# Spread's evacuation order, the first transfers and the last block's halves in a two-block transformer kernel

## The chip, the cores and the metric

The kernel runs on one core of one Trainium2 chip. The metric is the device time of one execution in microseconds (us). Five engines work side by side, each through its own queue in order: TensorE (PE) multiplies into PSUM, VectorE (DVE) and ScalarE (ACT) compute on SBUF and PSUM, GpSimd (POOL) and SyncE (SP) issue transfers here. SyncE and ScalarE both issue transfers between HBM and SBUF. [...]

## The reference, cut to what matters

The program computes two transformer blocks over 512 tokens of width 1024 in fp32. The first is norm, projections, chunked attention and a gated convolution, an output projection and a feed-forward part. The second is a modulated mixer and PEER, a layer of 16384 experts of which each token picks 128. The parts that the change touches are the very first projection and PEER:

```python
def rms_norm(x, g):
    y = xf * lax.rsqrt(jnp.mean(xf * xf, axis=-1, keepdims=True) + EPS)
    return (y * g.astype(jnp.float32)).astype(x.dtype)
...
h = rms_norm(x, norm1_g)
proj = jnp.einsum('bsd,de->bse', h, w_in)
...
# peer: 8 heads pick 16 of 128 keys twice, then 16 of the 256 pairs
idx = best_i.reshape(nb, PEER_TOKEN_BLOCK, n_sel)      # expert = i * 128 + j
gs = gate.reshape(nb, PEER_TOKEN_BLOCK, n_sel)
u = jnp.take(expert_u, ib, axis=0)
act = jax.nn.gelu(jnp.einsum('td,tkd->tk', xb, u).astype(jnp.float32), approximate=False)
vv = jnp.take(expert_v, ib, axis=0)
return jnp.einsum('tk,tkd->td', (gb * act).astype(h.dtype), vv)
```

## The kernel before

Every fp32 product of a weight and an activation is made of three matmuls: both factors are split into a high part (fp32r) and a low part, and `mm3` (lines 154 to 156) multiplies high by high, low by high and high by low. A weight tile of 1 MB comes in by one transfer on SyncE (`weights`, line 140), ScalarE makes the high part (line 143, one copy of 128x2048), VectorE the low part (line 145). The tile framework orders the instructions of each engine by its own schedule; what the change moves is told below. Each transfer takes one of eight semaphores in turn, and the one that takes a semaphore again waits for the transfer that had it, so that no more than eight of SyncE's and ScalarE's transfers are under way.

**Start.** `setup` loads two constants (`cst`, an identity and a block of ones, line 89; `vec`, all gains and biases, line 91) on SyncE. `block1` then takes the eight tiles of x (transposed, 128x512, line 285) on SyncE and the first weight in eight pieces of 128x256 on ScalarE (line 286), a piece and a tile at a time. For each, ScalarE multiplies x with its gain out of `vec` (line 229, the high part `hh`), VectorE makes the low part `lh` (line 230), ScalarE casts the weight's piece (line 289), VectorE makes its low part (line 290). The first 48 matmuls (`linear2`, both 128-column halves of a piece, piece by piece) need both; the next 48 use the weight `w_in[20]`, which comes in one transfer. Then come the column sums of x squared (lines 220 and 221).

**Spread.** For 384 of the 512 tokens every expert is computed densely, and the gates are laid out as a matrix of experts by tokens. `spread` makes that matrix: for 16 tokens at a time VectorE builds one-hot rows of the two keys (`oi` for i, `oj` for j, lines 1328 and 1330) and of j times the gate's high and low half (`oh`, `ol`, lines 1332 and 1334), each with two buffers. Per token PE multiplies `oh` by `oi` and adds `ol` by `oi` (lines 1340 and 1341), 128x128 each, four tokens in a bank; the banks are taken in turn from three tags (`c` and `d` with one bank, `b` with two, which also takes the transposes at the head of each block of 128 tokens). ScalarE copies a bank into `stage` (line 1343), a tile of 128 keys j by 128 keys i by 32 tokens, and after 32 tokens `stage` goes to HBM (line 1349, 2 MB). 96 copies are made. Between them, `ahead` computes the first 48 expert chunks' activations: 80 steps of six matmuls here, with their weights' casts (lines 143 and 145) and a gelu per chunk on ScalarE. After spread come the remaining steps of `ahead`, then the token rows (line 1101) and the first loads of gates (line 1396) and activations (line 1387) for `experts`.

**End.** `experts` walks 128 chunks. `products` (lines 1435, 1436 and 1439) adds six matmuls per chunk and block of 128 tokens, three for each half of the 1024 output columns. The last four chunks are taken block by block for the three blocks; behind each block, `tail` multiplies each half's sum with the second gate (line 1423), adds x (line 1424) and stores it (line 1425).

Of the kernel before, what the change touches and what calls it, by code (L numbers as in the profile page):

```python
# [8 lines left out]
F32 = mybir.dt.float32  # L9
# [12 lines left out]
P = 128  # L22
# [47 lines left out]
class Ker:  # L70
# [12 lines left out]
    def setup(self, es):  # L83
        nc, I = self.nc, self.I
        self.cp = es.enter_context(self.pool("cp"))
        self.raws = None
        self.table, self.table_load, self.table_users = None, None, []
        cst = self.cp.tile([P, 2 * P], F32, name="cst")
        nc.sync.dma_start(cst, I["consts"][:, 0:2 * P])
        vec = self.cp.tile([P, V_W], F32, name="vec")  # L90
        nc.sync.dma_start(vec, I["vecs"])
        self.vec = vec
        self.ident, self.bone = cst[:, 0:P], cst[:, P:2 * P]
        self.ones = self.cp.tile([P, P], F32, name="ones")
        nc.vector.memset(self.ones, 1.0)
        self.mod = self.cp.tile([P, 48], F32, name="mod")

    def act(self, out, x, func, **kw):
# [165 lines left out]
    def block1(self, es_x):  # L264
# [5 lines left out]
        with ExitStack() as es:  # L270
# [9 lines left out]
            with self.pool("n1") as tp:  # L280
                x0, hs = [], []
                raw, hi, lo = self.weight_tiles()
                for k in range(KO):
                    xt = tp.tile([P, T], F32, name=f"x0_{k}")
                    nc.sync.dma_start(xt, I["x"][k])
                    nc.scalar.dma_start(raw[:, k, :], I["w_in"][16][:, k, :])
                    x0.append(xt)
                    hs.append(self.gain_tile(hp, xt, self.v(V_N1 + k), "h1", KO))
                    nc.scalar.copy(hi[:, k, :], raw[:, k, :])
                    nc.vector.tensor_sub(lo[:, k, :], raw[:, k, :], hi[:, k, :].bitcast(F32))  # L290
                nc.vector.tensor_scalar_mul(bgh, self.v(V_BG, 16), 0.5)
                pcs = self.linear2((hi, lo), hs)
                pxs = self.linear2(self.weights(I["w_in"][20]), hs)
                acc = None
                for k in range(KO):
                    acc = self.sum_sq(tp, acc, x0[k])
                self.rsqrt(tp, self.col_sums(acc), 1.0 / D, out=rstd)
                nc.vector.tensor_mul(rstd2, rstd, rstd)
                pt = self.psum("c", 1)
                for i in range(4):  # L300
                    nc.tensor.transpose(pt[:, i * P:(i + 1) * P], rstd[:, i * P:(i + 1) * P], self.ident)
                nc.vector.tensor_copy(rtok, pt.rearrange("p (a b) -> p a b", b=P)[:, :, 0])
# [992 lines left out]
    def spread(self, kp, Ix, Jx, gate, g_dram, ahead, fetch):  # L1295
# [5 lines left out]
        with self.pool("oh", bufs=2) as tp:  # L1301
# [5 lines left out]
            for tb in range((TD + P - 1) // P):  # L1307
                if tb == 1:
                    next(fetch)
                pt = self.psum("b", 2)  # L1310
                for i, src in enumerate((Ix, Jx, gate)):
                    t = nc.tensor.transpose(pt[:, i * P:(i + 1) * P], src[:, tb, :], self.ident)
                    if tb == 0:
                        self.behind(t, after)
                ij = tp.tile([P, 2, P, 2], F16, name="oh_t")
                nc.scalar.copy(ij.rearrange("p a b c -> p (a b) c"), pt[:, :2 * P].unsqueeze(2).to_broadcast([P, 2 * P, 2]))
                gs = tp.tile([P, P], F32, name="oh_g", bufs=1)
                nc.scalar.activation(gs, pt[:, 2 * P:3 * P], AF.Copy, scale=2.0 ** 14)
                gh = tp.tile([P, 2, P, 2], F16, name="oh_w", bufs=1)
                gs = gs.unsqueeze(2).to_broadcast([P, P, 2])  # L1320
                nc.vector.tensor_copy(gh[:, 0], gs)
                nc.vector.tensor_sub(gh[:, 1], gs, gh[:, 0])
                for t0 in range(0, min(P, TD - tb * P), G):
                    if t0 % TB == 0:
                        stage = tp.tile([P, P, TB], F32, name="oh_s")
                    bc = lambda t: t[:, t0:t0 + G].unsqueeze(2).to_broadcast([P, G, P // 2, 2])
                    oi = tp.tile([P, G, P], F16, name="oh_i", bufs=2)
                    nc.vector.tensor_tensor(rows(oi), iota, bc(ij[:, 0]), op=ALU.is_equal)
                    oj = tp.tile([P, G, P], F16, name="oh_j", bufs=2)
                    nc.vector.tensor_tensor(rows(oj), iota, bc(ij[:, 1]), op=ALU.is_equal)  # L1330
                    oh = tp.tile([P, G, P], F16, name="oh_h", bufs=2)
                    nc.vector.tensor_mul(rows(oh), rows(oj), bc(gh[:, 0]))
                    ol = tp.tile([P, G, P], F16, name="oh_l", bufs=2)
                    nc.vector.tensor_mul(rows(ol), rows(oj), bc(gh[:, 1]))
                    for f in range(G // 4):
                        pg = self.psum("cdb"[nb % 3])
                        nb += 1
                        for i in range(4 * f, 4 * f + 4):
                            o = pg[:, (i % 4) * P:(i % 4 + 1) * P]
                            nc.tensor.matmul(o, oh[:, i, :], oi[:, i, :], start=True, stop=False)  # L1340
                            nc.tensor.matmul(o, ol[:, i, :], oi[:, i, :], start=False, stop=True)
                        o = t0 % TB + 4 * f
                        nc.scalar.activation(stage[:, :, o:o + 4].rearrange("p i t -> p t i"),  # L1343
                                             pg.rearrange("p (t i) -> p t i", t=4), AF.Copy, scale=2.0 ** -14)
                        n = (tb * P + t0) // 4 + f
                        for _ in range((n + 1) * left // (TD // 4) - n * left // (TD // 4)):
                            next(ahead, None)
                    if (t0 + G) % TB == 0:
                        nc.sync.dma_start(g_dram[(tb * P + t0) // TB], stage)
# [6 lines left out]
    def experts(self, es, hs, x_dram, g_dram, a_dram, rows):  # L1356
# [67 lines left out]
                nc.vector.tensor_add(o, t, o)  # L1424
                nc.sync.dma_start(self.y[b][:, half * T:(half + 1) * T], o)

        def products(b, n, v):

            mm = nc.tensor.matmul
            bc = slice(b * P, (b + 1) * P)  # L1430
            hi, lo = (t[:, bc] for t in ws[n])
            c = n % 2
            for half in range(2):
                hc = slice(half * T, (half + 1) * T)
                mm(sums[b][half], hi, v[0][:, c, hc], start=n == 0, stop=False)  # L1435
                mm(sums[b][half], hi, v[1][:, c, hc], start=False, stop=False)  # L1436
            for half in range(2):
                hc = slice(half * T, (half + 1) * T)
                mm(sums[b][half], lo, v[0][:, c, hc], start=False, stop=n == P - 1)  # L1439

# [19 lines left out]
            down_weights(p)  # L1460
        for _ in rows:
            pass
        for b in range(nb):
            for n in range(last, P):
                products(b, n, down[n // 2])
            tail(b)


def _tiled(w, ko=KO):
# [77 lines left out]
```

## Time and profile before

| what | value |
|---|---|
| median of 3 runs | 2550.01 us (2549.26 to 2550.56) |
| the profiled execution | 2545.76 us, its span 2544.0 us |
| PE busy | 2478.2 us, 97% of the span |
| DVE busy | 1868.4 us, 73% |
| ACT busy | 1098.0 us, 43% |
| PE's first matmul | 7.59 us |
| the 96 copies of spread | 1502.59 to about 1647 us |
| PE's last matmul ends | about 2538.3 us |

The page gives busy time by engine, the span in 40 slices, the chain of work that ended last, and the costliest groups of instructions; a group's line number is that of the source. The trace can be asked for the instructions of any stretch in order, for waits (who waited for whom, in total, how often, and the longest), and for each engine's busy time in a stretch. All times in it are from the profiled execution. Engines are idle in front of an instruction until what it waits for is there; the releaser stands behind an arrow.

### The profile page before, as it was taken

The numbers are of one execution on the slowest core, as the hardware profiler recorded it, in microseconds if no ns is written. First come the engines' busy times: TensorE is split into PE (matmuls) and PEld (weight loads), VectorE is DVE, ScalarE is ACT, GpSimd is POOL, SyncE is SP. The second block draws the span as 40 slices with busy tenths as digits, with TensorE's granted clock in tenths as the row PEclk, the third lists the DMA queues.
The fourth block names the chain that finished last, engine by engine and source line by source line (L and its number), as shares of the span: only waits on it lengthen the run. The fifth ranks groups of instructions, "written<-read, shape, count | busy, mean of one in ns | idle before, by whom it ended". The sixth has DMA issues, their size and how long they took to land. (4 is left out here: it accounts for less than half of the span.)

```text
span 2544.0 us, 33077 instructions
## 1 busy us (share of the span) xinstructions
PE 2478.2 (97%) x12637; PEld 2114.3 (83%) x12637; DVE 1868.4 (73%) x3094; ACT 1098.0 (43%) x1479; POOL 627.2 (25%) x506
## 2 busy tenths in 40 slices
PE   8999999999999999999999998999999999999999
PEld 6887887877888878777788987878889999999998
DVE  5558777755555557896779998767767877888887
ACT  5226555643222136666643357743333333333332
POOL 0001100111001001101045630011145555555552
PEclk9999999999999999999999999999999999999999
DMA  5353222443443441114343456799879999999995
GB/s 196 131 197 101 100 92 100 152 167 145 157 151 138 149 137 68 55 54 159 111 155 116 127 221 250 279 332 335 300 261 331 329 330 328 332 327 333 331 334 188
DMA packets 172312, 515.03 MB, mean 202 GB/s; under 512 B 13396, under 2 KB 78308, under 8 KB 146296
## 3 DMA queue, kind: packets, MB, share of 16 engines
q1 hardware_dynamic: 133960, 376.52, 41.9%
q0 software_dynamic: 37040, 135.35, 14.8%
q8 instruction: 99, 1.62, 0.2%
q10 hardware_dynamic: 1152, 1.05, 0.1%
q14 instruction: 61, 0.50, 0.1%
HBM read 461.47 MB, written 51.38 MB: 202 GB/s over the span
## 5 line engine op out<-in xcount | busy, mean ns | idle before, releaser
L143 ACT CAST whi<-wraw 128x2048 fp32r<-128x2048 f32 x229 | 437.7, 1911 | 545.2 <-PE pa L155 315.8
L145 DVE TENSOR_TENSOR wlo<-wraw,whi 128x2048 fp32r<-128x2048 f32 x210 | 489.0, 2329 | 131.4 <-ACT whi L143 126.5
L154 PE MATMUL pa<-hh,whi 128*128 128x512 f32 (+1 forms) x1360 | 522.6, 384 | 12.4 <-ACT hh L229 10.5
L155 PE MATMUL pa<-lh,whi 128*128 128x512 f32 (+1 forms) x1360 | 520.5, 383 | 0.0
L156 PE MATMUL pa<-hh,wlo 128*128 128x512 f32 (+1 forms) x1360 | 517.7, 382 | 1.2 <-DVE wlo L290 1.2
L1145 POOL DMA_INDIRECT r_row<-in_u_rows,r_at x128 | 190.2, 1486 | 467.2 <-DVE r_w L1166 430.6
L154 PEld LDWEIGHTS pa<-hh,whi 128*128 128x128 f32 x1360 | 256.3, 189 | 57.3 <-ACT hh L229 10.9
L1435 PE MATMUL pp<-whi,hew 128*128 128x512 f32 x768 | 299.2, 391 | 3.0 <-ACT whi L143 1.6
L1436 PE MATMUL pp<-wlo,hew 128*128 128x512 f32 x768 | 299.7, 391 | 1.4 <-DVE wlo L145 1.4
L155 PEld LDWEIGHTS pa<-lh,whi 128*128 128x128 f32 x1360 | 256.3, 188 | 44.0 <-issue 6.1
L156 PEld LDWEIGHTS pa<-hh,wlo 128*128 128x128 f32 x1360 | 255.9, 188 | 43.6 <-issue 3.6
L1145 POOL DMA_INDIRECT r_row<-in_expert_v,r_at x128 | 195.1, 1524 | 175.8 <-DVE r_big L1174 139.4
L1439 PE MATMUL pp<-whi,lew 128*128 128x512 f32 x768 | 237.2, 390 | 0.0
L154 PE MATMUL pu<-hh,whi 128*128 128x384 f32 x640 | 217.0, 339 | 0.0
L156 PE MATMUL pu<-hh,wlo 128*128 128x384 f32 x640 | 216.7, 339 | 0.0
L155 PE MATMUL pu<-lh,whi 128*128 128x384 f32 x640 | 216.4, 338 | 0.0
L1435 PEld LDWEIGHTS pp<-whi,hew 128*128 128x128 f32 x768 | 144.1, 188 | 32.2 <-ACT whi L143 2.1
L1439 PEld LDWEIGHTS pp<-whi,lew 128*128 128x128 f32 x768 | 144.1, 188 | 30.3 <-DVE lew L1403 0.2
L1436 PEld LDWEIGHTS pp<-wlo,hew 128*128 128x128 f32 x768 | 144.0, 188 | 29.8 <-DVE wlo L145 1.8
L1174 DVE SCALAR_TENSOR_TENSOR r_big<-r_row,r_w,r_big 128x1024 f32<-128x1024 f32 x127 | 162.9, 1283 | 3.0
L1402 ACT CAST hew<-ex_w 128x384 fp32r<-128x384 f32 x128 | 65.5, 513 | 228.7 <-DVE ex_w L1398 144.6
L1166 DVE CUSTOM_DVE_ANT_0 r_row<-r_row,r_big 128x1024 f32<-128x1024 f32 x128 | 151.3, 1220 | 0.0
(437 smaller groups left out, 4515.4 us busy)
## 6 DMA issues: line engine op xcount, KB each, us to landing
wraw<-in_expert_u SPq DMA_DIRECT2D x64, 1024.0 KB, 7.3
wraw<-in_expert_v SPq DMA_DIRECT2D x64, 1024.0 KB, 7.6
wraw<-in_w_in SPq DMA_DIRECT2D x37, 1024.0 KB, 4.8
ada_w<-in_w_ada SPq DMA_DIRECT2D x24, 1024.0 KB, 4.8
gate_dram<-oh_s SPq DMA_DIRECT2D x12, 2048.0 KB, 7.2
ex_g<-gate_dram SPq DMA_DIRECT2D x31, 768.0 KB, 11.3
wraw<-in_w_up SPq DMA_DIRECT2D x16, 1024.0 KB, 6.0
wraw<-in_w_down SPq DMA_DIRECT2D x16, 1024.0 KB, 4.7
```

What stands on the lines that cost most here:

```text
L143: nc.scalar.copy(hi, raw)
L145: nc.vector.tensor_sub(lo, raw, hi.bitcast(F32))
L154: mm(out, wh, xh, start=start, stop=False)
L155: mm(out, wh, xl, start=False, stop=False)
L156: return mm(out, wl, xh, start=False, stop=stop)
L1145: self.nc.gpsimd.indirect_dma_start(t, None, src, at)
L1166: later(nc.vector.tensor_tensor_reduce(row, row, h, 1.0, 0.0, op0=ALU.mult, op1=ALU.add, accum_out=w[:, k:k + 1]))
L1174: later(nc.vector.scalar_tensor_tensor(acc, row, w[:, k:k + 1], acc, op0=ALU.mult, op1=ALU.add))
L1402: nc.scalar.copy(hi, w)
L1435: mm(sums[b][half], hi, v[0][:, c, hc], start=n == 0, stop=False)
L1436: mm(sums[b][half], hi, v[1][:, c, hc], start=False, stop=False)
L1439: mm(sums[b][half], lo, v[0][:, c, hc], start=False, stop=n == P - 1)
```

## The change

Four things are changed.

1. **Evacuation in spread.** The copy from a PSUM bank to `stage` is the same 512 values, walked in another order: before, token by token with the 128 keys innermost (PSUM read in order, one value written every 128 bytes); after, key by key with the four tokens innermost (PSUM read with 512 bytes from value to value, four neighbouring values written, then a jump of 128 bytes to the next four).
2. **First transfers.** SyncE takes x's first tile, then `vec`, then the other seven tiles, then `cst`. The gains and casts stand in a loop of their own behind all transfers. A copy of one column of ones is put on ScalarE at the head.
3. **Products of ones at first.** Nine fp32 matmuls of the 128x128 tile of ones by itself go into a PSUM bank before the first real matmul; nothing reads them.
4. **Last block's halves in turn.** For the third block of tokens the last four chunks are taken for the first 512 columns, then for the other 512.

```diff
-        nc.sync.dma_start(cst, I["consts"][:, 0:2 * P])
         vec = self.cp.tile([P, V_W], F32, name="vec")
-        nc.sync.dma_start(vec, I["vecs"])
+        self.fixed = ((vec, I["vecs"]), (cst, I["consts"][:, 0:2 * P]))
...
         nc.vector.memset(self.ones, 1.0)
+        nc.scalar.copy(self.cp.tile([P, 1], F32, name="first"), self.ones[:, 0:1])
...
                 raw, hi, lo = self.weight_tiles()
+                pt = self.psum("c", 1)
+                for _ in range(9):
+                    nc.tensor.matmul(pt[:, :P], self.ones, self.ones, start=True, stop=True)
                 for k in range(KO):
                     xt = tp.tile([P, T], F32, name=f"x0_{k}")
                     nc.sync.dma_start(xt, I["x"][k])
                     nc.scalar.dma_start(raw[:, k, :], I["w_in"][16][:, k, :])
                     x0.append(xt)
+                    if k == 0:
+                        nc.sync.dma_start(*self.fixed[0])
+                nc.sync.dma_start(*self.fixed[1])
+                for k, xt in enumerate(x0):
                     hs.append(self.gain_tile(hp, xt, self.v(V_N1 + k), "h1", KO))
...
-                        nc.scalar.activation(stage[:, :, o:o + 4].rearrange("p i t -> p t i"),
-                                             pg.rearrange("p (t i) -> p t i", t=4), AF.Copy, scale=2.0 ** -14)
+                        nc.scalar.activation(stage[:, :, o:o + 4], pg.rearrange("p (t i) -> p i t", t=4), AF.Copy,
+                                             scale=2.0 ** -14)
...
-        def products(b, n, v):
+        def products(b, n, v, halves=(0, 1)):
...
-            for half in range(2):
+            for half in halves:
...
-        for b in range(nb):
+        for b in range(nb - 1):
             for n in range(last, P):
                 products(b, n, down[n // 2])
             tail(b)
+        for half in range(2):
+            for n in range(last, P):
+                products(nb - 1, n, down[n // 2], (half,))
+        tail(nb - 1)
```

On ScalarE at the start, the order with the semaphores that a row waits for (`DMAHW` and a number is one of the eight of the transfers, `wraw` a piece of the first weight, `hh` a gain). Before:

```order
L286 DMA wraw<-in_w_in 128x256 x4
L286 DMA wraw<-in_w_in 128x256 [waits DMAHW0_49]
L289 ACT_TABLE_LOAD
L289 CAST whi<-wraw 128x256
L229 ACTIVATE hh_97<-x_0_94,vec 128x512 [waits DMAHW5_49,DMAHW3_49]
L229 ACTIVATE hh_106<-x_1_103,vec 128x512 [waits DMAHW7_49]
L289 CAST whi<-wraw 128x256 [waits DMAHW2_49]
```

The same place after. The semaphores 0, 1, 3, 5 and 6 are there those of x's first tile, the first piece, x's second tile, x's third tile and the third piece; 2 is that of `vec`.

```order
L289 DMA wraw<-in_w_in 128x256
L95 ACT_TABLE_LOAD
L95 COPY first<-ones 128x1 [waits DVE_49]
L289 DMA wraw<-in_w_in 128x256 x2
L289 DMA wraw<-in_w_in 128x256 [waits DMAHW0_49]
L289 DMA wraw<-in_w_in 128x256 [waits DMAHW1_49]
L289 DMA wraw<-in_w_in 128x256 [waits DMAHW3_49]
L289 DMA wraw<-in_w_in 128x256 [waits DMAHW5_49]
L289 DMA wraw<-in_w_in 128x256 [waits DMAHW6_49]
L229 ACTIVATE hh_130<-x_0_104,vec 128x512 [waits DMAHW2_49]
L296 CAST whi<-wraw 128x256
```

All eight pieces' transfers stand ahead of the first gain now, and five of them wait for an earlier transfer; before, five stood there, one of them with a wait, and three came among the gains.

On VectorE at the end of the program, the last block's rows (`ex_t` is the sum times the gate, `y2` the block's rows of x). Before:

```order
L1423 TENSOR_TENSOR ex_t_21829<-pp_15073,y4_14943 128x512
L1423 TENSOR_TENSOR ex_t_21833<-pp_15074,y4_14943 128x512
L1424 TENSOR_TENSOR y2_14941<-ex_t_21829,y2_14941 128x512
L1424 TENSOR_TENSOR y2_14941<-ex_t_21833,y2_14941 128x512
L1543 UNCONDITIONAL_BRANCH
```

After, with `pp_15085` the first half's sum and `pp_15086` the second's:

```order
L1430 TENSOR_TENSOR ex_t_21841<-pp_15085,y4_14955 128x512
L1431 TENSOR_TENSOR y2_14953<-ex_t_21841,y2_14953 128x512
L1430 TENSOR_TENSOR ex_t_21845<-pp_15086,y4_14955 128x512
L1431 TENSOR_TENSOR y2_14953<-ex_t_21845,y2_14953 128x512
L1554 UNCONDITIONAL_BRANCH
```

The first half's two rows stand together now, ahead of the second half's. PE's last 24 matmuls are the same, the 12 of the first half ahead of the 12 of the second. In spread no row changes its place on any engine; only the shape of ScalarE's 96 copies does, from 128x4x128 to 128x128x4.

## Rows read from the trace of the kernel before

**Rows 1.** The page's first part: busy time of the engines, share, instructions.

```profile
PE 2478.2 (97%) x12637; PEld 2114.3 (83%) x12637; DVE 1868.4 (73%) x3094; ACT 1098.0 (43%) x1479; POOL 627.2 (25%) x506
```

**Rows 2.** Stretches: length, busy us of each engine (instructions), granted clock, DMA, GB/s.

```profile
0.00:12.00 12.00, 4.41 (x10) 3.19 (x11) 4.99 (x11) 6.64 (x12) 0.55 (x6) 1.00 0.79 264
12.00:34.00 22.00, 20.78 (x89) 16.12 (x88) 12.42 (x16) 12.38 (x18) 0.20 (x2) 1.00 0.47 170
34.00:100.00 66.00, 66.00 (x290) 53.76 (x289) 40.18 (x46) 22.14 (x21) 8.24 (x9) 1.00 0.44 162
1495.00:1647.00 152.00, 134.68 (x1242) 122.44 (x1241) 132.32 (x113) 117.80 (x131) 5.54 (x4) 1.00 0.68 268
1690.00:2544.00 854.00, 848.47 (x4153) 757.96 (x4151) 665.14 (x734) 288.83 (x302) 371.82 (x247) 1.00 0.89 314
```

**Rows 3.** Groups on ACT by shape: count, busy us, mean ns, idle before.

```profile
L1343 ACT ACTIVATE oh_s<-pc 128x512 f32<-128x512 f32 x32 | 36.7, 1146 | 9.9 <-PE pc L1341 4.6 <-issue 3.5 <-ACT ex_a L110 1.0
...
L1343 ACT ACTIVATE oh_s<-pd 128x512 f32<-128x512 f32 x32 | 35.8, 1120 | 8.6 <-PE pd L1341 8.6
...
L1101 ACT COPY y<-pu 128x512 f32<-128x512 f32 x10 | 5.6, 587 | 1.9 <-PE pu L1100 1.9
```

**Rows 4.** PE's waits from 1495 to 1662 us: total, times, longest.

```profile
PE pd L1340 <- ACT oh_s L1343: 8.9, 15, 1.3
PE pc L1340 <- ACT oh_s L1343: 6.1, 14, 0.7
```

**Rows 5.** DVE's waits from 1495 to 1647 us.

```profile
DVE oh_i L1328 <- PE pc L1341: 6.8, 4, 3.7
DVE oh_i L1328 <- PE pd L1341: 3.6, 2, 3.3
DVE oh_w L1321 <- ACT oh_g L1318: 2.6, 1, 2.6
```

**Rows 6.** In order of time, PE in spread: start, us, what, idle before it.

```profile
1503.71 0.22 PE L1340 MATMUL pc<-oh_i,oh_h 128*128 128x128 f16 x1 [0.38 <-ACT oh_s L1343]
```

**Rows 7.** Groups on DVE by shape: sums over runs of 8 and 4 fp16.

```profile
L1223 DVE TENSOR_TENSOR tk_e<-tk_e 128x2048 f16<-128x2048 f16 x4 | 7.8, 1948 | 0.1
...
L1223 DVE TENSOR_TENSOR tk_e<-tk_e 128x1024 f16<-128x1024 f16 x4 | 5.9, 1480 | 0.1
```

**Rows 8.** In order of time, the first 35 us, of several engines.

```profile
0.84 0.17 DVE L95 MEMSET ones<- 128x128 f32 x1 [0.84 <-PEq L1539]
...
1.67 6.60 SPq L285 DMA_DIRECT2D x<-in_x  x8
...
6.82 0.72 ACT L229 ACTIVATE hh<-x,vec 128x512 fp32r<-128x512 f32 x1 [1.04 <-DMA x<-in_x]
...
7.59 0.80 PE L154 MATMUL pa<-hh,whi 128*128 128x512 f32 x1 [7.59 <-ACT hh L229]
7.77 0.72 ACT L229 ACTIVATE hh<-x,vec 128x512 fp32r<-128x512 f32 x1 [0.23 <-DMA x<-in_x]
...
10.13 0.33 ACTq L286 DMA_DIRECT2D wraw<-in_w_in  x1
...
12.18 0.40 PE L155 MATMUL pa<-lh,whi 128*128 128x512 f32 x1
...
16.39 0.41 ACT L289 CAST whi<-wraw 128x256 fp32r<-128x256 f32 x1 [3.60 <-DMA wraw<-in_w_in]
...
33.78 1.02 PE L220 MATMUL pa<-cs_a,ones 128*128 128x512 f32 x2
```

**Rows 9.** PE behind an idle stretch in the second block, and its granted clock.

```profile
1046.39 0.80 PE L543 MATMUL pd<-sb_wh,vv 128*128 128x512 f32 x1 [3.36 <-DVE sb_wh L864]
...
1047.00:1048.00 1.00, 1.00 (x3) 0.50 0.00 0
```

**Rows 10.** In order of time, DVE behind PE's last matmul.

```profile
2538.28 1.29 DVE L1423 TENSOR_TENSOR ex_t<-pp,y 128x512 f32<-128x512 f32 x2 [2.95 <-PE pp L1439]
2539.49 1.28 DVE L1424 TENSOR_TENSOR y<-ex_t,y 128x512 f32<-128x512 f32 x2
```

More of the change, by code (lines that the diff above doesn't have):

```diff
@@ L1436, in products @@
                 mm(sums[b][half], hi, v[1][:, c, hc], start=False, stop=False)
-            for half in range(2):
+            for half in halves:
                 hc = slice(half * T, (half + 1) * T)
```

## The prediction

> **What bounds the kernel now.** I read the page's busy shares first, then a table of stretches, then the waits and the order of time in the three places that the diff touches. TensorE (PE) is busy 97% of the span [rows 1], and the stretches tell where it is not: from 34 to 100 us it never stops, from 1690 to the end it works 848.5 of 854 us, but it has 7.6 us without work before its first matmul, loses more until 34 us, and works only 134.7 of the 152 us in which spread runs [rows 2]. So the time is PE's, and a change is worth what it takes out of PE's gaps, at the start, in spread, and behind the last matmul. The weights stream at 314 GB/s in the last stretch without holding PE up [rows 2].
>
> **Spread's evacuation.** 96 times ScalarE (ACT) copies a PSUM bank of 512 values into the stage. Now it reads in order and writes each value 128 bytes from the last one: 1146 and 1120 ns a copy; a copy of the same size that writes in order takes 587 ns [rows 3]. The changed form writes runs of four values (16 bytes) and reads PSUM with 512 bytes from value to value. Same values, same count, same place in every queue.
> The write side: no ACT row writes such runs. The nearest are VectorE (DVE) sums over every second run: 2048 values in runs of 16 bytes take 1948 ns, 1024 values in runs of 8 bytes still 1480 [rows 7]; halving the run saves a quarter, so it is runs that cost there, and runs of 16 bytes stay under a nanosecond per value. I take the write as cured.
> The read side is the open price: no row reads many values across PSUM. Its lower end is 587 ns; as upper end I take what the write costs now, about 1130 ns, since one value per step across SBUF is the nearest thing the rows show. I take 590 to 650. Nothing in the rows shows PSUM slower than SBUF to an engine that takes one value at a time, and TensorE fills those banks with 512 values every 0.23 us (66.00 us for 290 matmuls [rows 2]), more than twice ACT's pace. That reason is thin, so the upper end stays in the range.
> [...]
> What it is worth: the copies release PE's banks. PE waits 8.9 + 6.1 = 15.0 us for them, in 29 waits of 0.52 us on average [rows 4]. A copy that is 0.5 us shorter closes such a wait: at 1503.71 it is one of 0.38 us behind a single copy [rows 6]. Where three copies stand in a row it takes off more. But then DVE is late, not PE: DVE needs 132.3 us of the same 152 [rows 2] against PE's 134.7, and has waited 6.8 + 3.6 us for PE to free its one-hot buffers and 2.6 us for a small ACT copy that stood behind four evacuations [rows 5], 13.0 in all. That bounds the gain from above: 13 us by DVE, 15 by PE. Weight casts stay in ACT's queue between the copies, so not every wait goes; I take three quarters of 13, **10 us**, bounds 0 and 14. The cover of DVE's passes is gone then: a pass that is late costs its full delay.
> The gain is not given back behind spread: the loads of gates and activations for the first expert chunks are queued behind the end of the same PE work and move with it, and afterwards PE is full.
>
> **The start.** Before: x's first tile is third in SyncE's queue, first issued at 1.67; ACT waits for it until 6.82, and PE starts at 7.59 at half pace (0.80 us for the first matmul, 0.40 for one at 12.18) [rows 8]. Three of the eight weight pieces were issued only from 10 us on, behind a 1 MB load, and the cast of one waits 3.6 us until 16.39 [rows 8]. PE has done the first two groups' 96 matmuls at 33.78; at 0.227 us each (66.00 for 290 [rows 2]) 21.8 us are work, so 33.78 - 7.59 - 21.8 = 4.4 us are losses: 2.1 of them are the slow pace up to 12 us (4.41 us for ten matmuls [rows 2], less 2.3), the rest waits.
> After: x's first tile and the vectors go first, so x lands sooner, but all eight pieces' transfers now stand in ACT's queue ahead of the first gain, and five of them have a semaphore of an earlier transfer to wait for (the order shows it): the seventh waits for the third x tile, the eighth for the third piece. That wait is **new**: the first gain and everything on ACT is queued behind it. The third x tile is fourth in SyncE's queue, where the second one was; that one had landed at 7.77 [rows 8], with 128 KB less ahead on its own queue and 256 KB more on ACT's. I take 6.5 to 7.8 for it, two issues of 0.33 behind [rows 8], the first gain at 7.2 to 8.5, and PE's start a gain (0.72) and a cast (0.39) later: 8.3 to 9.6, so 0.7 to 2.0 us **later** than before. What comes back: no piece is issued late any more (2.6 us), and the clock may be up. [...] So the clock's 2.1 us are a toss. In all the 96 matmuls end between 30.1 and 33.5 instead of 33.78; the load of the next weights has its cover (they are cast by about 20 us and needed then). **Gain 2.2**, bounds 0.3 and 3.7. Moved constants, the early table load and the copy of one column cost ACT 1.3 us at a time when it waits for transfers anyway: nothing.
>
> **The end.** The last block's two sums end together now, so DVE does two products and two sums behind the last matmul: 1.29 + 1.28 us less their overlap, 2538.28 to 2540.77, four passes of some 0.62 us [rows 10]. After, the first half is through 12 matmuls (2.7 us) earlier, its passes run under the second half's matmuls, and two passes are left: 1.2 us less. The number of matmuls is the same, twelve in a row go into one bank, as 24 do elsewhere. **Gain 1.2**, bounds 0.6 and 1.3.
>
> **The sum.** 10 + 2.2 + 1.2 = 13.4 us. The profiled execution took 2545.76 with a span of 2544.0; it would take 2532.4. The median of the runs is 2550.01, 4.25 above, so the forecast is **2536.6 us**. About 0.2% (5 us) is what a measurement of this kernel can tell from no change.
>
> **Rivals.**
> (a) The read pays what the write paid. Each value of a copy then costs as now, the copies stay near 1130 ns, PE's 15 us of waits stay, and only start and end gain: 2550 - 3.4 = **2546.6**, within 0.2% (2544 to 2549). For it: one value per step is dear on the SBUF side, 1146 against 587 ns [rows 3]. Against: another memory. [...]
> (b) The copies get short, but DVE's passes, or the casts in ACT's queue, hold the stage: of the 13 us some 4 come back. 2550 - 4 - 3.4 = **2542.6**. For it: DVE and PE have nearly the same work in spread [rows 2].
> (c) Slower: the read across PSUM costs more than the write did. The second step per value costs 0.55 us a copy (1146 less 587); if the read costs yet another, the copies go from 1.13 to 1.6 us with as much more between their starts, 0.45 to 0.5 us. That is 43 us more for ACT, which is busy 117.8 of 152 [rows 2], and the 29 waits, behind one to three copies, each grow by about 0.9: 26 us. 2550 + 26 - 3.4 = **2573**. It decides as soon as a copy takes longer than now.
> (d) The start does not do what it says: the eighth issue is held beyond 9 us, the products of ones warm a clock that has fallen again. That costs 1 to 2 us in place of the gain and shifts any case by 3 to 4: 2540 in the forecast's, 2550 in (a)'s; it decides none alone.
>
> **How the numbers follow.** Forecast (2530 to 2541): 0.53. (b): 0.15. (a): 0.25. (c): 0.07. The predicted time is the first case's. The range goes from 2529.5 (14 + 3.7 + 1.3 = 19, and 1.5 to spare) to 2548.5, which takes in most of (a); (c) and the tail of (a) with a bad start are left out, some 0.15. Faster by over 0.2% are the first case, nearly all of (b) and the best of (a): 0.70; slower is (c) with a trace of (d): 0.07; the rest, 0.23, is within.
>
> **What would show it.** Evacuation: the mean of the 96 copies, near 600 or near 1130 ns, settles (a), (b) and (c). Then PE's waits for them should fall from 15 us to under 4, DVE's waits for PE from 11 to a few, and the stretch from the first one-hot pass to PE's last product ahead of the experts shrink by 10. If copies are short and that stretch is not, (b) is right and a new releaser stands on PE's list. Start: ACT's first gain at 7 to 8.5 us behind its own eighth issue, PE's 96 matmuls through by 31; whether the first ones take 0.43 or 0.23. End: one product and one sum behind the last matmul. I am wrong in kind if the evacuation is as slow as now, or if the stage between 1647 and 1690 gives the gain back by waiting for transfers that did not move.

## The result, and the profile after

The changed kernel takes 2521.52 us (median of 4 runs, 2520.22 to 2523.94) against 2549.64 (2548.71 to 2550.56) beside it: ratio 0.9897, 95% interval 0.9885 to 0.9908. That is 28 us, twice what was forecast, and below the forecast's range. The profiled execution took 2522.37 us, 23.4 less than that of before.

The page's first part of the changed kernel, which answers [rows 1]:

```profile
PE 2467.9 (98%) x12655; PEld 2114.4 (84%) x12655; DVE 1872.7 (74%) x3094; ACT 1056.6 (42%) x1480; POOL 624.1 (25%) x506
```

PE has 18 more instructions, the products of ones (each is recorded as two), and yet 10 us less busy time. A change that only closes gaps would leave the busy time as it was; this is the first sign of something that the forecast did not have.

Stretches of the changed kernel, to be laid beside [rows 2] (length, busy us of PE, PEld, DVE, ACT, POOL, granted clock, DMA, GB/s):

```profile
0.00:12.00 12.00, 7.58 (x26) 6.66 (x27) 4.07 (x10) 5.96 (x12) 0.55 (x6) 0.86 0.82 271
12.00:34.00 22.00, 22.00 (x95) 17.49 (x94) 12.99 (x19) 14.39 (x19) 0.20 (x2) 1.00 0.56 197
1300.00:1495.00 195.00, 188.23 (x1028) 175.95 (x1027) 181.00 (x850) 68.26 (x79) 118.34 (x88) 0.98 0.39 130
1495.00:1647.00 152.00, 148.57 (x1333) 137.50 (x1331) 133.14 (x113) 80.82 (x136) 3.45 (x4) 0.99 0.75 294
1690.00:2520.60 830.60, 826.01 (x4092) 740.03 (x4090) 654.35 (x720) 283.25 (x296) 364.33 (x245) 1.00 0.90 317
```

The stretch ahead of spread, the selection of keys, in the kernel before:

```profile
1300.00:1495.00 195.00, 194.65 (x1054) 180.18 (x1052) 178.00 (x851) 69.47 (x80) 117.57 (x90) 1.00 0.41 134
```

The clock column is to be read with care at the start: it shows 1.00 for 0 to 12 us in [rows 2], where the first matmul took 0.80 us against 0.40 for one at 12.18 [rows 8], because the trace has no clock record before 11.9 us. In the 152 us that held spread before, PE now works 148.57 in place of 134.68: 13.9 us more. In the selection it works 6.4 us less than before: a new gap. And behind 1690, where only the last chunks' order was changed and PE is full in both, its busy time per matmul fell from 0.2043 us (848.47 for 4153, [rows 2]) to 0.2019 (826.01 for 4092).

The evacuation's copies by shape on ScalarE, which answer [rows 3]:

```profile
L1350 ACT ACTIVATE oh_s<-pc 128x512 f32<-128x512 f32 x32 | 19.3, 603 | 14.1 <-PE pc L1348 11.6 <-issue 2.5
L1350 ACT ACTIVATE oh_s<-pd 128x512 f32<-128x512 f32 x32 | 19.3, 602 | 10.4 <-PE pd L1348 10.2 <-ACT ex_a L110 0.2
```

603 ns in place of 1146, and ACT waits for PE where PE waited for ACT. PE's waits, first from 1300 to 1500 us, then from 1495 to 1662, which answers [rows 4]:

```profile
PE pb L1319 <- DVE pk_i L1236: 6.8, 1, 6.8
```

```profile
PE pd L1347 <- ACT oh_s L1350: 1.0, 1, 1.0
```

15.0 us of waits for copies have become 1.0. The one long wait is new: PE stands at the head of spread until VectorE has the keys (`pk_i`). VectorE's waits from 1495 to 1647 us, which answer [rows 5]:

```profile
DVE wlo L145 <- ACT whi L143: 4.9, 1, 4.9
DVE oh_i L1335 <- ACT oh_t L1323: 2.9, 3, 2.3
DVE oh_w L1328 <- ACT oh_g L1325: 0.9, 1, 0.9
```

Its 10.4 us of waits for PE are gone.

At the start, in order of time, the rows that answer [rows 8]: the first gain, the first matmul, and the column sums behind the first 96.

```profile
7.52 0.72 ACT L229 ACTIVATE hh<-x,vec 128x512 fp32r<-128x512 f32 x1 [4.85 <-DMA wraw<-in_w_in]
...
8.59 1.22 PE L154 MATMUL pa<-hh,whi 128*128 128x512 f32 x2 [3.36 <-ACT whi L296]
...
32.02 1.02 PE L220 MATMUL pa<-cs_a,ones 128*128 128x512 f32 x2
```

At the end, VectorE behind the last matmul, for [rows 10]: one product and one sum.

```profile
2516.05 0.69 DVE L1430 TENSOR_TENSOR ex_t<-pp,y 128x512 f32<-128x512 f32 x1 [1.30 <-PE pp L1446]
2516.78 0.69 DVE L1431 TENSOR_TENSOR y<-ex_t,y 128x512 f32<-128x512 f32 x1
```

Laying the starts of the same instructions in both traces side by side gives where the 23.4 us came from: +1.8 by 40 us, -1.0 from there to 640, +2.8 between 640 and 960, -4.9 between 1430 and 1500 (VectorE's starts; PE, which is further ahead there, waits), some +14 in spread, +8.1 between 1750 and 2500, +1.2 at the end (the rest is small). The gains between 640 and 960 and between 1750 and 2500 are in code that the change does not touch, and there each matmul is a few ns shorter.

### The profile page after: what moved, and what is told of

Its sections match the earlier page's. It is cut to its first block, busy times and chain, and to the rows that moved or that the text cites. A ratio compares the mean times of both kernels' runs of the same rounds, so it can differ in the third digit from the quotient of the medians.

```text
span 2520.6 us, 33112 instructions
## 1 busy us (share of the span) xinstructions
PE 2467.9 (98%) x12655; PEld 2114.4 (84%) x12655; DVE 1872.7 (74%) x3094; ACT 1056.6 (42%) x1480; POOL 624.1 (25%) x506
## 4 chain that ended last, share of the span: by engine, by line
PE 76%; DVE 15%; ACT 4%; DMA 2%; issue 2%; SPq 0%; POOL 0%; ACTq 0%; DVEq 0%; POOLq 0%
PE pa L154 12%; PE pa L156 12%; PE pa L155 12%; PE pp L1443 7%; PE pp L1442 7%; PE pp L1446 7%; PE pu L154 4%; PE pu L156 4%; PE pu L155 4%; DVE wlo L145 1%; ACT whi L143 1%; DVE tk_rest L1194 1%; PE pb L596 1%; DVE tk_e L1230 1%; DMA mg_a<-g_dram 1%
## 5 line engine op out<-in xcount | busy, mean ns | idle before, releaser
L1152 POOL DMA_INDIRECT r_row<-in_u_rows,r_at x128 | 184.4, 1440 | 461.7 <-DVE r_w L1173 419.6
## 6 DMA issues: line engine op xcount, KB each, us to landing
ex_g<-gate_dram SPq DMA_DIRECT2D x31, 768.0 KB, 10.9
```

The lines of the kernel that those rows point to most:

```text
L1152: self.nc.gpsimd.indirect_dma_start(t, None, src, at)
```

## Experiments: addresses

One thing differs for those matmuls. The changed kernel's `first` is a new tile of 4 bytes behind `ones`, and in the compiled program every tile that is allocated behind it stands 32 bytes further. Weights (`whi`, `wlo`) stood on multiples of 64 bytes before and now stand 32 beyond one. The activations (`hh`, `lh`) of the first block's feed-forward part and of the experts are allocated from SBUF's far end; they stand 32 beyond a multiple of 64 in both kernels.

**The tile alone.**

```diff
-        nc.vector.memset(self.ones, 1.0)
+        nc.vector.memset(self.ones, 1.0); self.cp.tile([P, 1], F32, name="first")
```

> The kernel before with one unused tile of 4 bytes a partition behind `ones`, as the change's `first` has it; it moves every tile that is allocated behind it by 32 bytes and changes no instruction. Theory S: a matmul whose activation tile and weight tile stand on different remainders of 64 bytes is slower (0.1767 instead of 0.1735 us for 384 columns, 0.232 instead of 0.227 for 512, in both traces), and the tile removes most such pairs. It takes 2.7 us between 620 and 960 us, 1.7 in spread and 8.3 behind 1690; the first part is lost in the selection, where VectorE is late, so about 10 us less: 2540 (2536 to 2542), the 128x384 group behind 1860 us at 336 ns. Rival R: the faster matmuls follow from something else in the change; then nothing happens, 2549.6, and that group stays at 339 ns.

2541.61 us against 2547.93, ratio 0.9972 (0.9961 to 0.9983): 7 us from a tile that nobody uses. In order of time on PE in the experts' stage, `pu` is a chunk's 24 matmuls of 384 columns, `pp` the 18 products of 512 columns behind them; the first of each, and the next chunk's first. The kernel before:

```profile
2099.71 0.34 PE L154 MATMUL pu<-hh,whi 128*128 128x384 f32 x1
...
2103.95 0.40 PE L1435 MATMUL pp<-whi,hew 128*128 128x512 f32 x1
...
2108.07 0.34 PE L154 MATMUL pu<-hh,whi 128*128 128x384 f32 x1
```

The kernel before with the tile:

```profile
2101.11 0.34 PE L154 MATMUL pu<-hh,whi 128*128 128x384 f32 x1
...
2105.28 0.39 PE L1435 MATMUL pp<-whi,hew 128*128 128x512 f32 x1
...
2109.37 0.34 PE L154 MATMUL pu<-hh,whi 128*128 128x384 f32 x1
```

24 matmuls take 4.17 in place of 4.24 us, a chunk 8.26 in place of 8.36; 80 chunks have them: 8 us. Theory S is right in kind. The whole gain is 7 and not 10 because this kernel has the new wait as well, and by VectorE's starts it loses 5.0 us between 1430 and 1500, more than it had gained before (its PE waits from 1300 to 1500 us):

```profile
PE pb L1312 <- DVE pk_i L1229: 6.8, 1, 6.8
```

**The other operand moved.** Here the weights stay and the activations move by 32 bytes.

```diff
-        self.cp = es.enter_context(self.pool("cp"))
+        self.cp = es.enter_context(self.pool("cp")); es.enter_context(self.pool("pad", side="right")).tile([P, 8], F32, name="pad")
```

> The kernel before with an unused tile of 32 bytes at the far end of SBUF, from where the activation tiles (`hh`, `lh`) are allocated downwards: these move by 32 bytes, the weights stay where they were in the kernel before, no instruction differs. Theory S2 (what counts is that the two operands of a matmul stand on the same remainder of 64 bytes): the 128x384 group behind 1860 us takes 336 ns as with the weights moved, and the gain is that of the 4-byte tile, 5 to 9 us: 2540 to 2543. Rival W (what counts is where the weights stand): 339 ns, no gain, 2548.

2540.47 against 2549.25, ratio 0.9971 (0.996 to 0.9983), and PE in order of time:

```profile
2102.82 0.39 PE L1435 MATMUL pp<-whi,hew 128*128 128x512 f32 x1
...
2106.91 0.34 PE L154 MATMUL pu<-hh,whi 128*128 128x384 f32 x1
...
2111.07 0.39 PE L1435 MATMUL pp<-whi,hew 128*128 128x512 f32 x1
```

4.16 us for the 24, and the same gain. It is not where the weights stand, but how the two operands of a matmul stand to each other. With each matmul's addresses taken from the compiled programs of six of these kernels (some 3000 matmuls of 384 columns in each; of 512 columns 5000 to 6400 with both operands on the same remainder and 200 to 1500 without), the median from one start to the next is 0.173 us for 384 columns where both operands stand on the same remainder of 64 bytes and 0.175 to 0.177 where they do not; for 512 columns it is 0.227, and 0.232 to 0.234.

**The changed kernel with the pair apart again.**

```diff
-        nc.scalar.copy(self.cp.tile([P, 1], F32, name="first"), self.ones[:, 0:1])
+        nc.scalar.copy(self.cp.tile([P, 16], F32, name="first")[:, 0:1], self.ones[:, 0:1])
```

> The changed kernel with a tile of 64 bytes for `first` in place of 4: all tiles behind it stand another 32 bytes further, so weights and activations are on different remainders of 64 bytes again; no instruction differs. Theory S: the gain of the shift goes, 2521.5 + 10 = 2531.5 (2529 to 2534), the 128x384 group behind 1860 us at 339 ns. Rival R: 2521.5, 336 ns.

2527.06, ratio 0.9915 (0.9898 to 0.9931): 2 to 6 us worse than the changed kernel's two sets (2521.52 and, below, 2524.93), less than the ten expected; the intervals overlap, so by its time alone this run shows little. PE in order of time:

```profile
2101.13 0.34 PE L154 MATMUL pu<-hh,whi 128*128 128x384 f32 x1
...
2105.37 0.39 PE L1442 MATMUL pp<-whi,hew 128*128 128x512 f32 x1
...
2109.45 0.34 PE L154 MATMUL pu<-hh,whi 128*128 128x384 f32 x1
```

The 24 take 4.24 again, as expected. But the products take 4.08, less than the 4.12 of before, and with the faster matmuls the 6.8 us wait is gone too (0.7 here): two reasons why only a part was lost.

**64 or 128 bytes.** The first experiment's tile with 96 bytes in place of 4.

```diff
-        ... self.cp.tile([P, 1], F32, name="first")
+        ... self.cp.tile([P, 24], F32, name="first")
```

> The kernel before with an unused tile of 96 bytes behind `ones`: the same remainder of 64 bytes as with 32, another one of 128. If 64 bytes is what counts, matmuls of 384 columns follow each other in 0.1730 us as with the 4-byte tile; if it is 128 bytes, in 0.175 to 0.177 us.

One execution, 2545.51. PE in order of time:

```profile
2102.18 0.33 PE L154 MATMUL pu<-hh,whi 128*128 128x384 f32 x1
...
2106.37 0.39 PE L1435 MATMUL pp<-whi,hew 128*128 128x512 f32 x1
...
2110.49 0.33 PE L154 MATMUL pu<-hh,whi 128*128 128x384 f32 x1
```

The median of 384 columns is 0.173, as with 32 bytes, but the first six of each 24 are slower (4.19 for the 24), and the products take 4.12. So the steady pace goes with the remainder of 64 bytes here, and there is a smaller part at the change from one kind of matmul to the other that it does not explain. What that is stays open.

## Experiments: evacuation, start and end

**The evacuation alone**, in the kernel before (the change's part 1).

```diff
-    ... stage[:, :, o:o + 4].rearrange("p i t -> p t i"),
-        pg.rearrange("p (t i) -> p t i", t=4), ...
+    ... stage[:, :, o:o + 4], pg.rearrange("p (t i) -> p i t", t=4), ...
```

> The kernel before with the new evacuation order alone. Theory S: the copies are 0.60 us, spread shrinks by 13 to 15 us, nothing else moves and the 128x384 group behind 1860 us stays at 339 ns: 2536 (2534 to 2538). Rival R, that the evacuation also speeds up the experts' matmuls (fewer stalls between transfers and stage): 2526 to 2528, the group at 336 ns.

2534.72 against 2547.93, ratio 0.9951 (0.9935 to 0.9968): 12.5 us by the ratio. Its stretch of spread and its 384-column group behind 1860 us:

```profile
1495.00:1647.00 152.00, 149.31 (x1330) 138.58 (x1329) 136.31 (x117) 81.69 (x136) 7.39 (x6) 0.99 0.77 299
```

```profile
L154 PE MATMUL pu<-hh,whi 128*128 128x384 f32 x593 | 201.1, 339 | 0.0
```

PE works 14.6 us more in the stretch; matmuls behind it are as before. Rival R falls.

**The old evacuation in the changed kernel** (the same lines turned round).

> The changed kernel with the old evacuation order. Theory S: copies of 1.13 us, PE's 15 us of waits for them are back, the shift's gain, the end's and what the start passes on remain: 2521.5 + 14 = 2535.5 (2533 to 2538). Rival R, that the evacuation carries nearly the whole gain: 2545 to 2547.

2537.59, ratio 0.9962 (0.9948 to 0.9976), 10 us under before where 14 were expected. Its copies and its PE's wait:

```profile
L1350 ACT ACTIVATE oh_s<-pc 128x512 f32<-128x512 f32 x32 | 36.9, 1153 | 9.8 <-PE pc L1348 4.5 <-issue 3.5 <-ACT ex_a L110 1.0
```

```profile
PE pc L1347 <- ACT oh_s L1350: 6.2, 14, 0.7
```

PE waits another 9.2 us for the copies of `pd`. What is left, 10 us (6 to 13 by the interval), holds the tile's 7; the other 3 may be start and end, which show 1 alone (below).

**A third order**, in the kernel before: two tokens innermost, then keys, then the other two tokens.

```diff
+    ... stage[:, :, o:o + 4].rearrange("p i (a b) -> p a i b", b=2),
+        pg.rearrange("p (a b i) -> p a i b", a=2, b=2), ...
```

> The kernel before with a third order of the evacuation: two tokens innermost, then the 128 keys, then the other two tokens, so that values are written in runs of 8 bytes and PSUM is read with the same 512 bytes from value to value. If the price is one per jump in SBUF, (1135 + 600)/2 with some rounding: 770 to 870 ns a copy. If a run must only be longer than one value: 600 ns. If runs under 16 bytes all pay alike: 1130 ns.

```profile
L1343 ACT ACTIVATE oh_s<-pc 128x512 f32<-128x512 f32 x32 | 20.5, 641 | 13.5 <-PE pc L1341 11.2 <-issue 2.3
```

One execution, 2530.22. 641 ns: a price per jump is refuted (770 to 870), a run of two values is nearly enough. Reading PSUM with 512 bytes from value to value costs at most 16 ns of a copy (603 against the 587 of [rows 3]). Runs of one, two and four values take 1146, 641 and 603 ns a copy. Rival (a), that the read pays what the write paid, falls with the 603.

**Start and end alone**, with the old evacuation and without `first`, so at the addresses of before.

> The kernel before with the new first transfers, the products of ones and the last block's halves, without the 4-byte tile `first` and with the old evacuation: addresses as before. The trace should show the 96 first matmuls through 1 to 2 us earlier, one product and one sum behind the last matmul, and matmuls of 339 ns. If start and end pass on what they gain: 3 us, 2545. If the start's part is lost before spread and only the end's 1.2 remains: 2546.7. Theory that the address is a small part and these two carry the rest of the 28: 2535 to 2538.

2548.26 against 2549.25, ratio 0.9996 (0.9986 to 1.0006): no difference that can be told, though the 3 us expected (0.9988) are just inside the interval. In its trace the first part of PE's work ends 1.5 us earlier than in [rows 8], and the end is as above. How far the start's part reaches can't be told from the traces: against that of before PE is 1.1 us ahead at 500 us and 2.8 behind at 640, in code that is the same in both and where traces differ anyway (more on this stretch with the offset, below). Through the selection nothing changes here (PE's longest wait there is 0.5). The theory that these two carry the rest falls.

**More products of ones.**

```diff
-                for _ in range(9):
+                for _ in range(22):
```

> The changed kernel with 22 products of ones in place of nine, so that they end near the first real matmul (9 took 4.17 us; from 1.06 us on, 22 end between 8 and 11). If the idle 3.36 us is what lets the clock fall, the first matmuls run at full pace and PE is through the first 96 about 1.5 us earlier than in the changed kernel, or later by what the products overrun; of the whole time nothing of it should remain, since the selection in front of spread waits for VectorE: 2521 within 2. Rival: the start's gain reaches the end, 2520 or less by the full 1.5.

2522.73, ratio 0.9894 (0.9878 to 0.9911): as the changed kernel. PE's stretch from 9 to 12 us, first of the changed kernel:

```profile
9.00:12.00 3.00, 3.00 (x8) 2.33 (x8) 3.00 (x8) 3.00 (x8) 0.00 (x0) 0.52 0.92 300
```

and of this one, with its first matmul and the wait in front:

```profile
8.78 0.49 PE L154 MATMUL pa<-hh,whi 128*128 128x512 f32 x1 [1.14 <-ACT whi L296]
```

```profile
9.00:12.00 3.00, 3.00 (x13) 2.25 (x13) 3.00 (x7) 3.00 (x7) 0.00 (x0) 1.00 0.96 339
```

13 matmuls in place of 8: behind an idle 1.14 us they start 0.23 us apart from 9.84 on (the clock column shows 1.00); behind 3.36 us they start 0.43 apart, with the clock at 0.52 over the stretch, near the 0.50 behind the 3.36 us of [rows 9]. Nine products are too few here: behind them the half pace (0.43 us) holds for seven matmuls in the changed kernel's trace and for eleven in the old evacuation's. The full pace is worth 1.2 us between executions that start alike (this one and the old evacuation's start at 8.78). Against the changed kernel's profiled execution, which starts 0.2 us earlier, the 96 are through only 0.2 us sooner, where 1.5 were expected. Of the whole time nothing is left, as expected.

## Experiments: what takes the gain back

Ahead of spread VectorE's short passes for the keys became long. By shape from 1428 to 1485 us, before:

```profile
L1229 DVE TENSOR_TENSOR pk_j<-tk_e 128x64 f32<-128x64 f16 x2 | 0.5, 308 | 0.0
L1229 DVE TENSOR_TENSOR pk_i<-tk_e 128x64 f32<-128x64 f16 x2 | 0.5, 298 | 0.0
```

and in the changed kernel:

```profile
L1236 DVE TENSOR_TENSOR pk_j<-tk_e 128x64 f32<-128x64 f16 x2 | 2.7, 1396 | 0.0
L1236 DVE TENSOR_TENSOR pk_i<-tk_e 128x64 f32<-128x64 f16 x2 | 2.5, 1284 | 0.0
```

GpSimd in order of time, before:

```profile
1435.96 8.59 POOL L149 TENSOR_TENSOR wlo<-wraw,whi 128x512 fp32r<-128x512 f32 x4 [4.09 <-ACT whi L143]
1446.20 5.05 POOL L149 TENSOR_TENSOR wlo<-wraw,whi 128x512 fp32r<-128x512 f32 x4 [1.66 <-ACT whi L143]
```

and in the changed kernel:

```profile
1429.58 16.49 POOL L149 TENSOR_TENSOR wlo<-wraw,whi 128x512 fp32r<-128x512 f32 x8 [1.97 <-ACT whi L143]
```

GpSimd makes the low parts of two weights here, in passes of 1.26 us from 1446.20 on (5.05 for four), of 2.06 on average in the 16.49 for eight. Before, it had finished the first weight when VectorE came to `pk_j` at 1445.56, and began the next at 1446.20. With faster matmuls PE frees the weights' tiles earlier (near 1433 us by 2.8 in the trace with the tile alone, where VectorE is 0.6 earlier), the cast follows, and GpSimd runs through. VectorE's passes for `pk_i` and `pk_j` stand beside them then and take about 1 us more each, 1.28 and 1.40 us on average for 0.30 and 0.31 before; the `MAX8` just ahead of them keeps its 0.28 (at 1440.89, and at 1445.64 in the trace with the tile alone). Why the two engines hold each other up is not shown.

That costs VectorE 3.4 of the 4.9 us. The other 1.5 come from PE's wait itself. All engines from 1486 to 1494 us, as in [rows 2], before and in the changed kernel:

```profile
1486.00:1494.00 8.00, 7.65 (x44) 7.20 (x43) 7.86 (x12) 5.55 (x6) 4.03 (x2) 1.00 0.16 20
```

```profile
1486.00:1494.00 8.00, 6.07 (x22) 5.97 (x23) 7.86 (x12) 0.60 (x1) 4.86 (x2) 0.57 0.25 65
```

Behind 6.77 idle us the clock is granted at 0.57 over this stretch, and PE's matmuls of 384 columns come every 0.32 us in place of 0.17 until 1493. VectorE's first one-hot rows, which follow behind a transpose in PE's queue, wait 2.3 us in place of 0.8.

**Two steps moved.**

```diff
-AH = (8, 8, 8, 8, 8, 8, 8, 40)
+AH = (8, 8, 8, 8, 8, 8, 6, 42)
```

> The changed kernel with two of the 40 steps of `ahead` around the seventh key head moved behind it (6 and 42 in place of 8 and 40). In the traces with the faster matmuls, GpSimd's low parts of two weights stand back to back from about 1430 us, VectorE's short passes beside them take 0.9 to 1.4 us instead of 0.3, and VectorE loses 5 us ahead of spread, for which PE then waits 6.8 us. If that collision is the cause and moving the weights' time parts them again, those 5 us come back: 2517 (2516 to 2519). If they collide elsewhere, or VectorE's queue is late for another reason: 2521 to 2524.

2518.14, ratio 0.9876 (0.9859 to 0.9892). The same passes, and PE's wait from 1300 to 1500 us:

```profile
L1236 DVE TENSOR_TENSOR pk_i<-tk_e 128x64 f32<-128x64 f16 x2 | 0.5, 294 | 0.0
L1236 DVE TENSOR_TENSOR pk_j<-tk_e 128x64 f32<-128x64 f16 x2 | 0.5, 261 | 0.0
```

```profile
PE pb L1319 <- DVE pk_i L1236: 2.9, 1, 2.9
```

Between 1430 and 1500 us VectorE loses 0.1 us against before, where in the changed kernel it loses 4.9. The collision is the cause of that loss.

**Both edits, and the changed kernel once more beside it.**

> The changed kernel with both edits: 22 products of ones, and two steps of `ahead` behind the seventh head. If VectorE is no longer late ahead of spread, what the warm clock saves at the start (1.2 us between executions with the same first matmul) reaches the end as well: 4 to 6 us under the changed kernel run beside it, some 2516.5. If the earlier start makes VectorE and GpSimd collide again in the selection: as the changed kernel, within 2 us.

> The changed kernel once more, unchanged, beside the next one on one chip. It should come out 26 to 29 us under the kernel before, with VectorE's passes for `pk_i` and `pk_j` near 1.3 us and PE's wait of 6.8 us ahead of spread.

The changed kernel: 2524.93 against 2550.41, ratio 0.9906 (0.9893 to 0.992), 25.5 us and so a little less than expected; PE's wait is 6.8 again, `pk_i` takes 1292 ns, and of `pk_j`'s two passes only one is long (850 on average). Both edits: 2516.63, ratio 0.9876 (0.9861 to 0.9891), 8.3 us under it where 4 to 6 were expected, the lowest median of this study. `pk_i` and `pk_j` take 260 and 286 ns in it. That the products add to it can't be told: with the moved steps alone the ratio is the same.

## Why the prediction was wrong

**Direction and mechanism** of the three parts were right; the time was not, by 15 us: 2536.6 forecast, 2521.5 measured. The parts of the sum:

- **A term that was not in the sum: +10.9, less 4.9.** "Moved constants, the early table load and the copy of one column cost ACT 1.3 us ...: nothing" priced the copy as an instruction and forgot its tile. The tile alone gives 7 us (e1's 0.9972). This is the step that failed first, the count of what the change moves: instructions and transfers were counted, addresses were not. The 10.9 are 2.8 and 8.1 in code that the change does not touch, the 4.9 the loss in the selection.
- **Evacuation, 10 forecast, 13.9 measured** (12.5 alone, by its ratio, 14.6 by its stretch). The read was rightly put at 590 to 650 (603), rivals (a), (b) and (c) fell, and the bound of 13 from VectorE's waits was nearly the value. That the write is cured came true by luck: "it is runs that cost there" misread [rows 7]. Three of the four passes of each size ran beside GpSimd, with 2176 to 2200 ns for 2048 values and 1709 to 1742 for 1024; the fourth, from 1485 to 1488 us, did not:

```profile
L1223 DVE TENSOR_TENSOR tk_e<-tk_e 128x2048 f16<-128x2048 f16 x1 | 1.2, 1226 | 0.0
L1223 DVE TENSOR_TENSOR tk_e<-tk_e 128x1024 f16<-128x1024 f16 x1 | 0.8, 750 | 0.0
```

The means of 1948 and 1480 lie 722 and 730 ns above these two, and say little of runs. What failed in the size was "I take three quarters of 13": the casts in ACT's queue, which should have kept a quarter, hold PE no longer once the copies are half as long, since ACT itself now waits for PE 11.6 + 10.2 us. The upper bound, 14, is about what came.
- **Start, 2.2 forecast, 1.8 measured** in the profiled execution. First gain 7.2 to 8.5: 7.52. First matmul 8.3 to 9.6: 8.59. The 96 through between 30.1 and 33.5: 32.02. The toss on the clock fell to "fallen again": the first seven matmuls start 0.43 us apart. No run shows what the 2.2 holds for the clock, an estimate of the author's; in its place the runs showed this pace behind nine products, and behind 22 the full one, worth 1.2 us. The reasoning on x's third tile had a sign wrong: its own queue has 128 KB more ahead of it than the second tile had (x's second tile, 256 KB, in place of `cst`, 128 KB), not less; the range was wide enough. Executions with the same transfers and nine products differ: in four others it was 0.7 to 1.5, and once 0.3 were lost (moved steps, first gain at 8.46).
- **"The gain is not given back behind spread ... and afterwards PE is full"** was right behind spread, and missed the place ahead of it. What faster matmuls give PE before 1430 us ends at VectorE's selection: PE was at 194.65 of 195 there, which looked like a PE-bound stage, while VectorE sat just under it. Whether the start's gain gets that far is not shown: with start and end alone PE is behind the trace of before at 640 us already, and the time is 0.9996 of before.
- **End, 1.2 forecast, 1.2 measured.**
- **From the profiled execution to the median, +4.25.** The forecast carried over that before's profiled execution was 4.25 under its median. The changed kernel's was 0.85 above its own. So that offset belonged to one execution: in the four sets before's runs go from 2544.9 to 2553.3. The traces differ by some 4 us between 500 and 640 us, in code that all kernels share, and there the profiled execution of before was a lucky one. PE (busy us, granted clock, DMA, GB/s) in it and in start and end alone:

```profile
500.00:640.00 140.00, 135.40 (x580) 1.00 0.46 162
500.00:640.00 140.00, 134.61 (x564) 0.98 0.45 160
```

The 16 matmuls between them are 3.6 us at 0.227. Twelve of the thirteen other traces have 0.98 or 0.99 there, the third order's 1.00. Whether this is the whole 4.25 is not shown, as runs that were not profiled have no trace. The offset made 5 of the 15.

15.1 is thus about 6 for addresses, 4 for spread, 5 for the offset. The range failed because its lower end was the sum of the known terms' best ends, with 1.5 us to spare for what was not in the sum.

## What to carry to other kernels

A new tile, however small, can change every address behind it (4 bytes moved them by 32 here): compile before and after, look at where the operands of the most frequent instruction stand to each other, and when a trace shows the same instruction faster in untouched code, try the tile alone. Write runs of at least two fp32 values to SBUF where an order can be chosen (641 ns a copy here, 1146 for single values). A stage in which one engine shows no wait can have a second one just under it; before pricing a gain ahead of such a stage, look for what ends it. Do not read a price from a group's mean before its passes have been looked at one by one: another engine may stand beside some of them. Nor carry the offset of one profiled execution over to the median of another kernel.

## Hardware behaviour that was not expected

- In six of these kernels a matmul's pace went with whether its two SBUF operands start on the same remainder of 64 bytes: 0.173 against 0.175 to 0.177 us for 384 columns, 0.227 against 0.232 to 0.234 for 512. Moving either operand by 32 bytes mended it (0.9972 and 0.9971).
- ScalarE read PSUM with 512 bytes from value to value nearly as fast as in order (603 and 587 ns for 512 values per partition); writing single values 128 bytes apart took nearly twice that (1146), pairs 641.
- VectorE's `pk_i` and `pk_j` passes, 0.30 and 0.31 us with GpSimd idle, took 1.28 and 1.40 on average beside its low parts (16.49 us for eight).
- Matmuls that put PE 2.8 us ahead near 1433 us (the tile alone) cost VectorE 5.0 us by 1500, through passes of GpSimd that moved beside its own (16.38 us for eight from 1433.15) and PE's wait of 6.8 us, behind which, in the changed kernel, the clock was granted at 0.57 from 1486 to 1494.
